# S5 states laid out by time, its input products side by side, its output weights in one half of the array

## The chip, the cores and the metric

The kernel runs on one core of a Trainium2 chip. The metric is the device time of one execution in microseconds (us). A core has a matrix engine (TensorE, PE in the profile), whose weight loads have a row of their own (PEld), a vector engine (DVE), a scalar engine (ACT), a general engine (POOL), and a queue engine (SP) that here only starts loads. Each engine takes its instructions strictly in the order of its own list, and waits when the next one's inputs or buffers are not ready.

## The reference, cut to what matters

Two identical layers run over 272 tokens (16 learned ones and 256 given) of width 2048. In each layer one input projection feeds three mixers: retention, gated linear attention (GLA) and S5. The change lies in the S5 branch alone, which is a complex recurrence over time:

```python
bu_re = jnp.einsum('blgc,gpc->blgp', ug, bb_re)
bu_im = jnp.einsum('blgc,gpc->blgp', ug, bb_im)
...
_, _, h_re, h_im = lax.associative_scan(complex_affine_combine, (a_re, a_im, bu_re, bu_im), axis=1)
y = jnp.einsum('blgp,gcp->blgc', h_re, c_re) - jnp.einsum('blgp,gcp->blgc', h_im, c_im)
return y.reshape(bsz, length, S5_WIDTH) + d * u
```

The index g runs over 64 groups of 16 channels, p over 64 complex states of a group, l over time.

## The kernel before

**Main products.** All large products are made from 656 chunks of weights (8 blocks of 128x128), which SP loads. ACT rounds a chunk to `hi` (L137), DVE makes the rest `lo` (L139), each with three buffers, and TensorE multiplies: L194, L195 and L196 in the first part of a layer, L191 and L196 where the activations' two halves are streamed together. A chunk is 24 products of the first kind. Every 16 or 8 weight blocks form one `acc` tile. These are called main products below.

**Order.** `schedule()` writes out the order of the output blocks by hand: GLA heads 0 and 1, the eight S5 input blocks (`su`), GLA heads 2 and 3, the retention heads (`rv`, `rk`, `rq`, `rg`), then gates and output. The smaller work is queued by `after(n, ...)`, which runs it n chunks later. A scheduler then places each engine's instructions, so what is traced together may stand apart on TensorE.

**S5.** Two time steps are folded into one, which leaves HALF = 136 steps, and two groups share the 128 partitions, which leaves 32 pairs. For each of the eight S5 blocks `s5_weights` turns the input weights (transposes into `tz`, copied out by ACT), and `s5_in` multiplies them with the inputs: 8 products for 4 pairs, each on 64 rows of the array (pr = 0 the lower half, pr = 1 the upper), into four PSUM tiles `s2p`. ACT copies each tile into the state tensor `H` (L537). When all of H is written, `s5_scan` runs the recurrence on POOL: 135 steps of three instructions, each on all 64 numbers (real and imaginary part of 32 pairs) of a partition: L543 multiplies the state of step n - 1 by the table `tab`, L545 and L546 add the two parts to step n. `s5_out` then multiplies H with the output weights `Ct`, 64 columns wide, into the PSUM tile `yp` (L558), behind one product with `K0` (L555); DVE adds the results to `su`. The scan has no other work in its way on POOL, and the products of `s5_out` stand in TensorE's list among the main products of the last retention heads.

`H` is [partition, time, re/im, pair] before. PSUM has five buffers for such small tiles (`patt`); `s2p`, `tz`, `yp`, and the small tiles of the other mixers share them.

Of the kernel before, what the change touches and what calls it, by code (L numbers as in the profile page):

```python
# [12 lines left out]
F32 = mybir.dt.float32  # L13
# [3 lines left out]
AF = mybir.ActivationFunctionType  # L17
ALU = mybir.AluOpType
# [4 lines left out]
P = 128  # L23
# [13 lines left out]
PAIRS = 32  # L37
HALF = T // 2
# [51 lines left out]
def hybrid(ctx: ExitStack, tc: tile.TileContext, xT, wst, wg, small, bcp, cst, rot, dec, out):  # L90
    nc = tc.nc
    V, S, G, PE = nc.vector, nc.scalar, nc.gpsimd, nc.tensor
# [3 lines left out]
    tp = ctx.enter_context(tc.tile_pool(name="tp", bufs=1))  # L96
# [6 lines left out]
    def nm(s):  # L103
        cnt[0] += 1
        return f"{s}_{cnt[0]}"

    def U(w=T):
        t = tp.tile([P, 288], F32, tag="u", name=nm("u"), bufs=NU)
        return t[:, :w]
# [4 lines left out]
    def PT(shape, s="att"):  # L114
        return patt.tile(shape, F32, tag="att", name=nm(s))
# [4 lines left out]
    def sm(l, n, i=None):  # L120
        a, b = SMALL[n]
        return smalls[l][:, a:b] if i is None else smalls[l][:, a + i:a + i + 1]
# [25 lines left out]
    def after(n, fn):  # L148

        cnt[0] += 1  # L150
        lag.append((state["t"] + n, cnt[0], fn))
# [22 lines left out]
    def bg_finish(g):  # L174
        if g in bg:
            for _ in g:
                pass
            bg.remove(g)

    def block(mv, nk, c0, wide=False):  # L180
        ps = pacc.tile([P, 512], F32, tag="acc", name=nm("acc"))
        w = T - c0
        both = wide and 2 * w <= 512
        for hc in range(nk // 8):
            prefetch(AHEAD + 1)
            hi, lo = chunks.popleft()
            for k in range(8):
                kk = hc * 8 + k
                o = ps[:, 0:w]
                if both:  # L190
                    PE.matmul(ps[:, 0:2 * w].rearrange("p (j t) -> p j t", j=2), hi[:, k, :], mv[:, :, kk, c0:T],  # L191
                              start=(kk == 0), stop=False, skip_group_check=True)
                else:
                    PE.matmul(o, hi[:, k, :], mv[:, 0, kk, c0:T], start=(kk == 0), stop=False)  # L194
                    PE.matmul(o, hi[:, k, :], mv[:, 1, kk, c0:T], start=False, stop=False)  # L195
                PE.matmul(o, lo[:, k, :], mv[:, 0, kk, c0:T], start=False, stop=(kk == nk - 1),  # L196
                          skip_group_check=both)
            bg_step()
        if both:
            z = U(w)  # L200
            S.activation(z, ps[:, w:2 * w], AF.Copy)
            V.tensor_tensor(out=ps[:, 0:w], in0=ps[:, 0:w], in1=z, op=ALU.add)
        return ps[:, 0:w]
# [90 lines left out]
    for d in range(0, KT, 4):  # L294
        if d < 12:
            tc.keep_in_program_order(S.activation(sq[:, d:d + 4, :], h0[:, d:d + 4, :], AF.Square))
        else:
            tc.keep_in_program_order(V.tensor_tensor(out=sq[:, d:d + 4, :], in0=h0[:, d:d + 4, :],
                                                     in1=h0[:, d:d + 4, :], op=ALU.mult))
# [24 lines left out]
    e = 1  # L324
# [3 lines left out]
    for l in range(DEPTH):  # L328
# [33 lines left out]
        s5 = {}  # L362
# [149 lines left out]
        su = tp.tile([P, NB, 2, HALF], F32, tag="su", name=nm("su"))  # L512
# [14 lines left out]
        def s5_in(b, u2):  # L527
            H = s5["H"]
            s2s = [PT([P, 2, HALF], "s2p") for _ in range(4)]
            for v_ in range(2):  # L530
                for ri in range(2):
                    for pr in range(2):
                        h_ = slice(64 * pr, 64 * pr + 64)
                        PE.matmul(s2s[2 * v_ + pr][:, ri, :], s5["ts", b][v_][h_, ri, :], u2[h_, v_, :], start=True,
                                  stop=True)
            for j, s2 in enumerate(s2s):
                S.activation(H[:, :, :, 4 * b + j].rearrange("p n r -> p r n"), s2, AF.Copy)  # L537

        def s5_scan():
            H, tab = s5["H"], s5["tab"]  # L540
            for n in range(1, HALF):
                pr = tp.tile([P, 2, 2, PAIRS], F32, tag="pr", name=nm("pr"), bufs=2)
                G.tensor_tensor(out=pr, in0=H[:, n - 1].unsqueeze(1).broadcast_to([P, 2, 2, PAIRS]),  # L543
                                in1=tab.rearrange("p (k r) q -> p k r q", k=2), op=ALU.mult)
                G.tensor_tensor(out=H[:, n], in0=H[:, n], in1=pr[:, 0], op=ALU.add)  # L545
                G.tensor_tensor(out=H[:, n], in0=H[:, n], in1=pr[:, 1, ::-1, :], op=ALU.add)  # L546
                if n % 2 == 0:
                    yield

        n0 = c0 // 2  # L550

        def s5_out(b):
            H, Ct, K0 = s5["H"], s5["C"], s5["K0"]
            yp = PT([P, 3, HALF], "yp")
            PE.matmul(yp[:, 2, n0:], K0[:, b, :], su[:, b, 0, n0:], start=True, stop=True, skip_group_check=True)  # L555
            m0 = max(n0 - 1, 0)
            for ri, q in ((0, 0), (0, 1), (1, 0), (1, 1), (0, 2), (0, 3), (1, 2), (1, 3)):
                PE.matmul(yp[64 * (q % 2):64 * (q % 2) + 64, q // 2, m0:],  # L558
                          Ct[:, ri, 4 * b + q].rearrange("p e a b -> p (e a b)"), H[:, m0:, ri, 4 * b + q],
                          start=(ri == 0), stop=(ri == 1), tile_position=(0, 64 * (q % 2)), skip_group_check=True)  # L560
            so = su[:, b, 0, n0:]
            V.scalar_tensor_tensor(out=so, in0=so, scalar=sm(l, "d", b), in1=yp[:, 2, n0:], op0=ALU.mult, op1=ALU.add)
            a = max(n0, 1)
            for q in range(4):
                r_, c_ = slice(32 * q, 32 * q + 32), 64 * (q % 2)
                so = su[r_, b, 1, n0:]
                V.scalar_tensor_tensor(out=so, in0=so, scalar=sm(l, "d", b)[r_], in1=yp[c_:c_ + 32, q // 2, n0:],
                                       op0=ALU.mult, op1=ALU.add)
                so = su[r_, b, 0, a:]
                V.tensor_tensor(out=so, in0=so, in1=yp[c_ + 32:c_ + 64, q // 2, a - 1:HALF - 1], op=ALU.add)  # L570
            so = su[:, b, :, n0:]
            S.activation(so, so, AF.Gelu_apprx_tanh)

# [191 lines left out]
        for kind, i, nk in schedule():  # L765
# [19 lines left out]
            elif kind == "su":  # L785
                if i == 0:
                    bg_finish(prep)
                    s5["H"] = tp.tile([P, HALF, 2, PAIRS], F32, tag="big", name=nm("H"))
                ps = block(x, nk, 0)
                V.tensor_tensor(out=su[:, i], in0=ps.rearrange("p (n e) -> p e n", e=2),  # L790
                                in1=R.rearrange("p (n e) -> p e n", e=2), op=ALU.mult)
                u2 = U().rearrange("p (a b) -> p a b", a=2)
                for v_ in range(2):
                    for pr in range(2):
                        for e in range(2):
                            G.dma_start(out=u2[64 * pr + 32 * e:64 * pr + 32 * e + 32, v_, :],  # L796
                                        in_=su[64 * v_ + 32 * pr:64 * v_ + 32 * pr + 32, i, e, :])
                after(3, partial(s5_weights, i))
                after(5, partial(s5_in, i, u2))
                if i == NB - 1:  # L800
                    scan = s5_scan()
                    after(6, partial(bg.append, scan))
            elif kind == "rv":
                if i == 0:
                    s2 = tp.tile([P, 2, NB, T], F32R, tag="s2", name=nm("ro"))
# [11 lines left out]
            elif kind == "rg":  # L817
                z = gate(block(x, nk, c0))
                after(5, partial(lambda z, rl, i: gated(z, rl["n"], s2, i), z, rl, i))
                if i == RH - 2:  # L820
                    after(6, partial(bg_finish, scan))
                    for b in range(NB):
                        after(6 + 3 * b // 2, partial(s5_out, b))
            elif kind == "sg":
# [9 lines left out]
                if i >= 4:  # L834
                    for b in (2 * i - 8, 2 * i - 7):
                        so_split(b)
                        so = su[:, b, :, n0:]
                        G.tensor_tensor(out=so, in0=so, in1=sgs[b][:, c0:].rearrange("p (n e) -> p e n", e=2),
                                        op=ALU.mult)
            elif kind == "glu":  # L840
                if i == 0:
# [4 lines left out]
                                in1=z[:, c0:].rearrange("p (n e) -> p e n", e=2), op=ALU.mult)  # L846
# [47 lines left out]
        else:  # L894
# [3 lines left out]
            r = U()  # L898
# [88 lines left out]
```

## Time and profile before

| what | value |
|---|---|
| time of three runs | 2164.37, 2166.74, 2167.22 us (median 2166.74) |
| profiled execution: time, and span of its instructions | 2164.37 us, 2162.6 us |
| TensorE's mean granted clock | 0.996 of full speed |
| busy: PE, DVE, ACT, POOL | 99%, 66%, 48%, 32% of the span |
| POOL, the three instructions of the scan | 457.7 us in all (169.6 + 152.1 + 136.0) |

The profiled execution is one of the three. TensorE's products are pipelined: in the rows, a product's duration includes its passage through the array, so that the next one begins long before it ends. What a product costs is read from the distance of the starts. A product of plain fp32 data (all of S5) shows as two passes, that is two records.

### The profile page before, as it was taken

How to read it: one execution, taken by the hardware profiler on the slowest of the kernel's cores; microseconds unless marked ns; L12 is line 12 of the kernel's file. 1: busy time of each engine (PE TensorE's matmuls, PEld its weight loads, DVE VectorE, ACT ScalarE, POOL GpSimd, SP SyncE). 2: the span in 40 equal slices, each digit the busy share in tenths (PEclk: the TensorE clock that was granted, in tenths of full speed). 3: DMA queues.
4: the chain of work that ended last, by engine and by line, in shares of the span. 5: the costliest groups of instructions: out<-in, count | busy, mean ns of one | idle time of the engine just before them, and what ended most of it. 6: DMA issues, size and time to landing. Idle time of an engine off the chain costs nothing. (4 is left out here: it accounts for less than half of the span.)

```text
span 2162.6 us, 39822 instructions
## 1 busy us (share of the span) xinstructions
PE 2140.4 (99%) x15650; PEld 2010.5 (93%) x15650; DVE 1434.2 (66%) x2370; ACT 1039.5 (48%) x1516; POOL 696.9 (32%) x1111
## 2 busy tenths in 40 slices
PE   9999999999999999999999999999999999999997
PEld 8999999998999999999999999999978888888886
DVE  7943788887555555555668636888886666666655
ACT  6655444446434444434445555444365444445454
POOL 3153888841200000002321428888603000000022
PEclk9999999999999999999999999999999999999999
DMA  6343444443555555545654434444435555555564
GB/s 225 141 156 120 153 165 161 161 147 106 178 176 176 176 174 174 173 173 192 213 204 149 150 125 160 163 170 163 152 109 184 190 189 187 191 187 188 191 212 152
DMA packets 108412, 365.47 MB, mean 169 GB/s; under 512 B 14016, under 2 KB 21696, under 8 KB 107968
## 3 DMA queue, kind: packets, MB, share of 16 engines
q1 hardware_dynamic: 101536, 353.73, 47.6%
q0 software_dynamic: 6400, 8.92, 1.3%
q8 instruction: 123, 2.02, 0.4%
q14 instruction: 65, 0.53, 0.1%
q10 hardware_dynamic: 288, 0.27, 0.1%
HBM read 356.32 MB, written 4.33 MB: 167 GB/s over the span
## 5 line engine op out<-in xcount | busy, mean ns | idle before, releaser
L137 ACT ACTIVATE hi<-raw 128x1024 fp32r<-128x1024 f32 x656 | 695.3, 1060 | 947.3 <-PE acc L195 533.0
L139 DVE TENSOR_TENSOR lo<-raw,hi 128x1024 fp32r<-128x1024 f32 x656 | 823.6, 1256 | 464.2 <-ACT hi L137 455.5
L196 PE MATMUL acc<-x,lo 128*128 128x272 f32 (+1 forms) x3840 | 1103.1, 287 | 1.1 <-DVE lo L139 1.1
L194 PE MATMUL acc<-x,hi 128*128 128x272 f32 (+1 forms) x2944 | 856.1, 291 | 1.1 <-ACT hi L137 1.1
L195 PE MATMUL acc<-x,hi 128*128 128x272 f32 (+1 forms) x2944 | 849.6, 289 | 0.0
L196 PEld LDWEIGHTS acc<-x,lo 128*128 128x128 f32 x3840 | 722.9, 188 | 4.3 <-DVE lo L139 1.5
L194 PEld LDWEIGHTS acc<-x,hi 128*128 128x128 f32 x2944 | 555.0, 189 | 11.8 <-issue 7.4
L195 PEld LDWEIGHTS acc<-x,hi 128*128 128x128 f32 x2944 | 555.2, 189 | 2.8
L191 PE MATMUL acc<-x,hi 128*128 128x512 f32 x896 | 316.0, 393 | 0.2 <-ACT u L756 0.2
L860 POOL TENSOR_TENSOR u<-u,u 128x272 f32<-128x272 f32 (+1 forms) x32 | 24.2, 755 | 768.2 <-DVE u L856 743.8
L191 PEld LDWEIGHTS acc<-x,hi 128*128 128x128 f32 x896 | 168.1, 188 | 41.2 <-issue 2.6
L543 POOL TENSOR_TENSOR pr<-H,tab 128x128 f32<-128x128 f32 x270 | 169.6, 628 | 78.6 <-ACT H L537 57.6
L545 POOL TENSOR_TENSOR H<-H,pr 128x64 f32<-128x64 f32 x270 | 152.1, 563 | 21.2
L196 PE MATMUL acc<-y,lo 128*128 128x272 f32 (+1 forms) x512 | 145.7, 285 | 0.0
L546 POOL TENSOR_TENSOR H<-H,pr 128x64 f32<-128x64 f32 x270 | 136.0, 504 | 21.2
L196 PEld LDWEIGHTS acc<-y,lo 128*128 128x128 f32 x512 | 96.3, 188 | 0.4
L191 PE MATMUL acc<-y,hi 128*128 128x512 f32 x240 | 83.8, 393 | 0.0
L796 POOL DMA_DIRECT2D u<-su x128 | 63.0, 500 | 52.6 <-ACT hi L137 31.5
L194 PE MATMUL acc<-y,hi 128*128 128x272 f32 (+1 forms) x272 | 78.4, 288 | 0.0
L195 PE MATMUL acc<-y,hi 128*128 128x272 f32 (+1 forms) x272 | 78.2, 288 | 0.0
L196 PE MATMUL acc<-ro,lo 128*128 128x272 f32 (+1 forms) x256 | 72.9, 285 | 0.0
L196 PE MATMUL acc<-go,lo 128*128 128x272 f32 (+1 forms) x256 | 72.9, 285 | 0.0
(285 smaller groups left out, 2726.2 us busy)
## 6 DMA issues: line engine op xcount, KB each, us to landing
raw<-wst SPq DMA_DIRECT2D x656, 512.0 KB, 3.3
h<-xT SPq DMA_DIRECT2D x8, 272.0 KB, 5.6
u<-su POOLq DMA_DIRECT2D x128, 17.0 KB, 2.5
u<-dec SPq DMA_DIRECT2D x16, 136.0 KB, 3.3
u<-xT POOLq DMA_DIRECT2D x16, 136.0 KB, 2.5
h<-u POOLq DMA_DIRECT2D x16, 136.0 KB, 2.2
u<-h POOLq DMA_DIRECT2D x16, 136.0 KB, 4.3
pre<-bcp SPq DMA_DIRECT2D x2, 1024.0 KB, 8.1
```

The source lines that it names most:

```text
L137: S.activation(hi, raw, AF.Copy)
L139: V.tensor_tensor(out=lo, in0=raw, in1=hi.bitcast(F32), op=ALU.subtract)
L191: PE.matmul(ps[:, 0:2 * w].rearrange("p (j t) -> p j t", j=2), hi[:, k, :], mv[:, :, kk, c0:T], start=(kk == 0), stop=False, skip_group_ch ...
L194: PE.matmul(o, hi[:, k, :], mv[:, 0, kk, c0:T], start=(kk == 0), stop=False)
L195: PE.matmul(o, hi[:, k, :], mv[:, 1, kk, c0:T], start=False, stop=False)
L196: PE.matmul(o, lo[:, k, :], mv[:, 0, kk, c0:T], start=False, stop=(kk == nk - 1), skip_group_check=both)
L543: G.tensor_tensor(out=pr, in0=H[:, n - 1].unsqueeze(1).broadcast_to([P, 2, 2, PAIRS]), in1=tab.rearrange("p (k r) q -> p k r q", k=2), op= ...
L545: G.tensor_tensor(out=H[:, n], in0=H[:, n], in1=pr[:, 0], op=ALU.add)
L546: G.tensor_tensor(out=H[:, n], in0=H[:, n], in1=pr[:, 1, ::-1, :], op=ALU.add)
L796: G.dma_start(out=u2[64 * pr + 32 * e:64 * pr + 32 * e + 32, v_, :], in_=su[64 * v_ + 32 * pr:64 * v_ + 32 * pr + 32, i, e, :])
L860: G.tensor_tensor(out=t[:, c0:], in0=t[:, c0:], in1=mg["y"][:, c0:], op=ALU.add)
```

## The change

In the S5 branch:

- `H` becomes [partition, re/im, pair, time], so that the 136 steps of one pair lie side by side, and the 64 numbers of one step lie 544 bytes apart (136 x 4). ACT's copies, the scan and the output products read and write it in that form.
- `s5_in` goes through v, ri, pr in another order (the upper row half first), and each product is pinned behind the one before it, so that the eight stand together on TensorE. `s5_weights` is queued one chunk earlier.
- `s5_out` takes two PSUM tiles instead of one. All its output weights go to columns 0 to 63 of the array; before, two of four pairs used columns 64 to 127.

```diff
-            for v_ in range(2):
-                for ri in range(2):
-                    for pr in range(2):
-                        h_ = slice(64 * pr, 64 * pr + 64)
-                        PE.matmul(s2s[2 * v_ + pr][:, ri, :], s5["ts", b][v_][h_, ri, :], u2[h_, v_, :], start=True,
-                                  stop=True)
+            for j, (v_, ri, pr) in enumerate((v_, ri, pr) for v_ in (1, 0) for ri in (0, 1) for pr in (1, 0)):
+                h_ = slice(64 * pr, 64 * pr + 64)
+                mm = PE.matmul(s2s[2 * v_ + pr][:, ri, :], s5["ts", b][v_][h_, ri, :], u2[h_, v_, :], start=True, stop=True)
+                if j:
+                    tc.keep_in_program_order(mm)
             for j, s2 in enumerate(s2s):
-                S.activation(H[:, :, :, 4 * b + j].rearrange("p n r -> p r n"), s2, AF.Copy)
+                S.activation(H[:, :, 4 * b + j, :], s2, AF.Copy)
...
-                G.tensor_tensor(out=pr, in0=H[:, n - 1].unsqueeze(1).broadcast_to([P, 2, 2, PAIRS]),
+                G.tensor_tensor(out=pr, in0=H[:, :, :, n - 1].unsqueeze(1).broadcast_to([P, 2, 2, PAIRS]),
                                 in1=tab.rearrange("p (k r) q -> p k r q", k=2), op=ALU.mult)
-                G.tensor_tensor(out=H[:, n], in0=H[:, n], in1=pr[:, 0], op=ALU.add)
-                G.tensor_tensor(out=H[:, n], in0=H[:, n], in1=pr[:, 1, ::-1, :], op=ALU.add)
+                G.tensor_tensor(out=H[:, :, :, n], in0=H[:, :, :, n], in1=pr[:, 0], op=ALU.add)
+                G.tensor_tensor(out=H[:, :, :, n], in0=H[:, :, :, n], in1=pr[:, 1, ::-1, :], op=ALU.add)
...
-            for ri, q in ((0, 0), (0, 1), (1, 0), (1, 1), (0, 2), (0, 3), (1, 2), (1, 3)):
-                PE.matmul(yp[64 * (q % 2):64 * (q % 2) + 64, q // 2, m0:],
-                          Ct[:, ri, 4 * b + q].rearrange("p e a b -> p (e a b)"), H[:, m0:, ri, 4 * b + q],
-                          start=(ri == 0), stop=(ri == 1), tile_position=(0, 64 * (q % 2)), skip_group_check=True)
+            for q in range(4):
+                for ri in range(2):
+                    PE.matmul(yps[q // 2][0:64, q % 2, m0:], Ct[:, ri, 4 * b + q].rearrange("p e a b -> p (e a b)"),
+                              H[:, ri, 4 * b + q, m0:], start=(ri == 0), stop=(ri == 1), skip_group_check=True)
...
-                    s5["H"] = tp.tile([P, HALF, 2, PAIRS], F32, tag="big", name=nm("H"))
+                    s5["H"] = tp.tile([P, 2, PAIRS, HALF], F32, tag="big", name=nm("H"))
...
-                after(3, partial(s5_weights, i))
+                after(2, partial(s5_weights, i))
```

On TensorE, the second S5 block of the first layer stood like this before; `s2p` is the result of `s5_in`, the second operand `u` its weights, `acc` rows are main products:

```order
L194 MATMUL acc_1816<-x_83,hi_1722 128x272
L534 MATMUL s2p_1750<-u_1529,u_1672 128x136
L534 MATMUL s2p_1751<-u_1529,u_1672 128x136
L534 MATMUL s2p_1750<-u_1529,u_1672 128x136
L534 MATMUL s2p_1751<-u_1529,u_1672 128x136
L195 MATMUL acc_1816<-x_83,hi_1722 128x272
L196 MATMUL acc_1816<-x_83,lo_1724 128x272
L194 MATMUL acc_1816<-x_83,hi_1722 128x272
L195 MATMUL acc_1816<-x_83,hi_1722 128x272
L534 MATMUL s2p_1752<-u_1529,u_1677 128x136 x2
```

Six of the block's eight products are seen: four with the row halves in turn, and two of one row half after four main products; the last two follow 15 main products later. The same block now (the products' line has moved up by two):

```order
L195 MATMUL acc_1826<-x_83,hi_1778 128x272
L532 MATMUL s2p_1763<-u_1539,u_1620 128x136
L532 MATMUL s2p_1762<-u_1539,u_1620 128x136
L532 MATMUL s2p_1763<-u_1539,u_1620 128x136
L532 MATMUL s2p_1762<-u_1539,u_1620 128x136
L532 MATMUL s2p_1761<-u_1539,u_1615 128x136
L532 MATMUL s2p_1760<-u_1539,u_1615 128x136
L532 MATMUL s2p_1761<-u_1539,u_1615 128x136
L532 MATMUL s2p_1760<-u_1539,u_1615 128x136
L521 MATMUL tz_1806<-cs,Z_871 128x128 x2
L196 MATMUL acc_1826<-x_83,lo_1780 128x272
```

All eight stand together, the row halves in turn. The last block of such products stands 12 main products later than its last piece did in the first layer (behind 1140 of them instead of 1128), and 13 later in the second (9016 instead of 9003); the second pair of transposes for the next block follows 12 main products behind each group.

The first output products of the first layer on TensorE, before:

```order
L196 MATMUL acc_5996<-x_83,lo_5964 128x272
L555 MATMUL yp_6060<-su_235,K_107_1363 128x136
L558 MATMUL yp_6060<-H_1372,C_1106 64x136 x8
L194 MATMUL acc_6086<-x_83,hi_5999 128x272
L195 MATMUL acc_6086<-x_83,hi_5999 128x272
```

And now:

```order
L196 MATMUL acc_5996<-x_83,lo_5964 128x272
L554 MATMUL yp_6060<-su_235,K_107_1363 128x136
L558 MATMUL yp_6060<-H_1372,C_1106 64x136 x4
L558 MATMUL yp_6061<-H_1372,C_1106 64x136 x4
L194 MATMUL acc_6087<-x_83,hi_5999 128x272
```

They have not moved: 3024 main products of the kernel stand ahead of them in both orders, and 10896 ahead of the second layer's. POOL's list is the same in both: the scan's rows follow the same transfers.

## Rows read from the trace of the kernel before

**Rows 1.** The page's first part: busy time of TensorE, share of the span.

```profile
PE 2140.4 (99%) x15650; PEld 2010.5 (93%) x15650; DVE 1434.2 (66%) x2370; ACT 1039.5 (48%) x1516; POOL 696.9 (32%) x1111
```

**Rows 2.** Timeline of PE: start, length, line, operation, count; an input burst of four passes.

```profile
124.70 0.29 PE L194 MATMUL acc<-x,hi 128*128 128x272 f32 x1
...
124.95 0.29 PE L196 MATMUL acc<-x,lo 128*128 128x272 f32 x1
125.17 0.73 PE L534 MATMUL s2p<-u,u 64*128 64x136 f32 x4
125.82 0.39 PE L194 MATMUL acc<-x,hi 128*128 128x272 f32 x1
126.06 0.29 PE L195 MATMUL acc<-x,hi 128*128 128x272 f32 x1
```

**Rows 3.** Timeline of PE: an input burst of eight passes.

```profile
138.14 0.73 PE L534 MATMUL s2p<-u,u 64*128 64x136 f32 x8
139.03 0.29 PE L196 MATMUL acc<-x,lo 128*128 128x272 f32 x1
```

**Rows 4.** Line L534: passes, shortest/median/longest ns, first and last start.

```profile
L534 PE MATMUL s2p<-u,u x256: 276/276/380, 125.2 to 1292.5; 64*128 64x136 f32 x128
```

**Rows 5.** Timeline of PE: the first output block of the first layer.

```profile
467.92 0.39 PE L555 MATMUL yp<-su,K 128*128 128x136 f32 x2
468.24 2.63 PE L558 MATMUL yp<-H,C 128*64 128x136 f32 x16
470.81 0.39 PE L194 MATMUL acc<-x,hi 128*128 128x272 f32 x1
```

**Rows 6.** Timeline of PE: the first two output blocks of the second layer.

```profile
1553.02 0.38 PE L555 MATMUL yp<-su,K 128*128 128x128 f32 x2
1555.62 2.51 PE L558 MATMUL yp<-H,C 128*64 128x129 f32 x16 [2.21 <-POOL H L546]
1558.06 0.58 PE L194 MATMUL acc<-x,hi 128*128 128x256 f32 x1
...
1561.79 2.51 PE L558 MATMUL yp<-H,C 128*64 128x129 f32 x16
1564.23 0.39 PE L194 MATMUL acc<-x,hi 128*128 128x256 f32 x1
```

**Rows 7.** Windows behind that wait: length, busy times, granted clock (PEclk), DMA.

```profile
1555.70:1559.10 3.40, 3.40 (x21) 2.52 (x22) 2.63 (x7) 0.00 (x0) 0.00 (x0) 0.51 0.52 181
1559.20:1565.00 5.80, 5.80 (x45) 4.51 (x44) 4.72 (x12) 3.11 (x4) 0.00 (x0) 1.00 0.10 39
```

**Rows 8.** The scan's three lines: count, shortest/median/longest ns, first and last start.

```profile
L543 POOL TENSOR_TENSOR pr<-H,tab x270: 453/464/1586, 199.7 to 1554.3; 128x128 f32<-128x128 f32 x135
L545 POOL TENSOR_TENSOR H<-H,pr x270: 317/325/1805, 200.7 to 1554.8; 128x64 f32<-128x64 f32 x135
L546 POOL TENSOR_TENSOR H<-H,pr x270: 317/324/1772, 201.1 to 1555.2; 128x64 f32<-128x64 f32 x135
```

**Rows 9.** Timeline of POOL: two neighbours, the first layer's last, the second's first.

```profile
300.24 0.33 POOL L546 TENSOR_TENSOR H<-H,pr 128x64 f32<-128x64 f32 x1
300.65 0.46 POOL L543 TENSOR_TENSOR pr<-H,tab 128x128 f32<-128x128 f32 x1
...
458.42 0.32 POOL L546 TENSOR_TENSOR H<-H,pr 128x64 f32<-128x64 f32 x1
...
1293.66 0.73 POOL L543 TENSOR_TENSOR pr<-H,tab 128x128 f32<-128x128 f32 x1 [29.62 <-ACT H L537]
```

**Rows 10.** Window over the first scan, of line L139 (`lo`) alone: DVE busy, count.

```profile
199.60:458.80 259.20, 99.95 (x76) 1.00 0.46 158
```

**Rows 11.** Groups of ACT by line: count, busy us, mean ns of one, idle before.

```profile
L137 ACT ACTIVATE hi<-raw 128x1024 fp32r<-128x1024 f32 x656 | 695.3, 1060 | 947.3 <-PE acc L195 533.0 <-issue 204.4 <-PE acc L191 189.3
L537 ACT ACTIVATE H<-s2p 128x272 f32<-128x272 f32 x64 | 40.4, 667 | 29.3 <-PE s2p L534 28.8
L523 ACT ACTIVATE u<-tz 128x256 f32<-128x256 f32 x32 | 11.1, 399 | 0.0
```

More of the change, by code (lines that the diff above doesn't have):

```diff
@@ L553, in s5_out @@
             H, Ct, K0 = s5["H"], s5["C"], s5["K0"]
-            yp = PT([P, 3, HALF], "yp")
-            PE.matmul(yp[:, 2, n0:], K0[:, b, :], su[:, b, 0, n0:], start=True, stop=True, skip_group_check=True)
+            yps = [PT([P, 3, HALF], "yp") for _ in range(2)]
+            PE.matmul(yps[0][:, 2, n0:], K0[:, b, :], su[:, b, 0, n0:], start=True, stop=True, skip_group_check=True)
             m0 = max(n0 - 1, 0)
-            for ri, q in ((0, 0), (0, 1), (1, 0), (1, 1), (0, 2), (0, 3), (1, 2), (1, 3)):
-                PE.matmul(yp[64 * (q % 2):64 * (q % 2) + 64, q // 2, m0:],
-                          Ct[:, ri, 4 * b + q].rearrange("p e a b -> p (e a b)"), H[:, m0:, ri, 4 * b + q],
-                          start=(ri == 0), stop=(ri == 1), tile_position=(0, 64 * (q % 2)), skip_group_check=True)
+            for q in range(4):
+                for ri in range(2):
+                    PE.matmul(yps[q // 2][0:64, q % 2, m0:], Ct[:, ri, 4 * b + q].rearrange("p e a b -> p (e a b)"),
+                              H[:, ri, 4 * b + q, m0:], start=(ri == 0), stop=(ri == 1), skip_group_check=True)
             so = su[:, b, 0, n0:]
-            V.scalar_tensor_tensor(out=so, in0=so, scalar=sm(l, "d", b), in1=yp[:, 2, n0:], op0=ALU.mult, op1=ALU.add)
+            V.scalar_tensor_tensor(out=so, in0=so, scalar=sm(l, "d", b), in1=yps[0][:, 2, n0:], op0=ALU.mult, op1=ALU.add)
             a = max(n0, 1)
             for q in range(4):
-                r_, c_ = slice(32 * q, 32 * q + 32), 64 * (q % 2)
+                r_, yp = slice(32 * q, 32 * q + 32), yps[q // 2][:, q % 2]
                 so = su[r_, b, 1, n0:]
-                V.scalar_tensor_tensor(out=so, in0=so, scalar=sm(l, "d", b)[r_], in1=yp[c_:c_ + 32, q // 2, n0:],
+                V.scalar_tensor_tensor(out=so, in0=so, scalar=sm(l, "d", b)[r_], in1=yp[0:32, n0:],
                                        op0=ALU.mult, op1=ALU.add)
                 so = su[r_, b, 0, a:]
-                V.tensor_tensor(out=so, in0=so, in1=yp[c_ + 32:c_ + 64, q // 2, a - 1:HALF - 1], op=ALU.add)
+                V.tensor_tensor(out=so, in0=so, in1=yp[32:64, a - 1:HALF - 1], op=ALU.add)
             so = su[:, b, :, n0:]
```

## The prediction

> **What bounds the kernel now.** I read the page's busy times first: TensorE is busy for 99% of the span [rows 1], so whatever its list loses or gains is the time, unless it is made to wait. Next came its timeline around the S5 products, to see what they cost between main products, which follow each other every 0.125 us (124.70 to 124.95 with one between) [rows 2]. Third, the list of who waited for whom and the rows behind it: TensorE waits once for the scan on POOL, 2.21 us in the second layer [rows 6]. The scan itself waits for nothing between its first and last instruction: neighbours are 0.08 us apart (300.24 + 0.33 to 300.65) [rows 9]. It runs from 199.7 to 458.74 in the first layer (259 us) and from 1293.66 to 1555.6 in the second (262 us) [rows 8, 9]; the output products want it at 468.24 and at 1553.4 [rows 5, 6]. So POOL is idle for two thirds of the span and yet has 9.5 us to spare in one layer and none in the other. That is what decides here.
>
> **Gain 1: the input products.** A burst of four passes on one row half takes 0.89 us from its first start to the second main product behind it (125.17 to 126.06) [rows 2]; a burst of eight with the halves in turn takes the same 0.89 (138.14 to 139.03) [rows 3], so the two halves work at once. Against the two main products' steps it would hold anyway, a burst costs 126.06 - 124.95 - 0.25 = 0.86 us [rows 2]. Four steps of 0.116 are in it (0.73 less the 0.276 of the last pass [rows 4], less the slower first step, over the rest); the other 0.39 is the way in and out, paid per burst. The 256 passes [rows 4] stand in 53 bursts, 42 of four and 11 of eight, counted over the timeline: 53 x 0.855 = 45.3 us. Now there are 16 bursts of 16 passes, eight pairs each: 0.86 + 4 x 0.116 = 1.33 us, 21.2 us in all. **Gain 24.1 us.** The transposes moved one chunk earlier stay the same transposes; the second pair of each block needs a PSUM tile that ACT's first copy of H frees, and 12 main products (1.5 us) stand ahead of it as cover, against one copy of about 0.4 us and at worst one `hi` of 1.06 us ahead of that [rows 11]. Without cover it would be 14 waits of up to 1 us; I take 0.
>
> **Gain 2: the output products.** Two passes of 64 columns run at once, eight pairs from 468.24 to 470.81: 2.57 us, 0.30 per pair and a way out [rows 5]. The K0 product, whose right side lies unbroken in SBUF, does a pass of the same length in 0.39 - 0.276 = 0.115 us [rows 4, 5]. [...] With H unbroken, 16 passes one after the other: 15 x 0.115 + 0.20 for the way out (as behind the input bursts: 125.17 + 0.73 - 0.276 to 125.82 [rows 2, 4]) = 1.93 us, or 1.80 with the second layer's shorter passes (0.38 for two K0 passes [rows 6]) against 2.44. **Gain 16 x 0.64 = 10.2 us.** If 64 columns no longer cost a way in and out, 0.29 us more per block, 4.6 in all.
>
> [...]
>
> **Off the path.** ACT's copies of H take 0.667 us each with their steps of 256 bytes; copies of the same kind out of `tz` take 0.399 for 256 elements, so 0.41 for 272 by the slope of `hi` ((1060 - 399) / 768 = 0.86 ns) [rows 11]. 64 x 0.25 us of ACT are saved, on an engine that waits for TensorE. DVE reads the same sizes from two tiles. Neither sets the end.
>
> **Loss: the scan.** POOL's scan starts when the last copy of H is done [rows 9], and I let TensorE's clock of main products tell what it has. The last input group stands 12 (13) main products later, 1.5 us, and is longer, with four copies behind it: I estimate that the scan starts 3 us after that burst's start, where it was 1.8 us. From scan start to `s5_out` this leaves 266 us in the first layer (268.5 before) and 257 in the second (259.7 before).
>
> A step of the scan is 0.464 + 0.325 + 0.324 by the medians [rows 8] and three gaps of 0.08: 1.35 us, 182 us for 135. The other 77 and 80 us are the long ones (up to 1.8 us), which I put down to DVE's `lo` operations, 76 in the first scan [rows 10], about 1 us each. So POOL has 182/259 = 0.703 and 182/262 = 0.696 of the time for itself, and within 266 and 257 us it can do 187 and 179 us of work. When TensorE waits, `lo` stops for want of buffers, and the rest runs free.
>
> Now each step reads H one number at a time, 544 bytes apart: 128 reads in L543 (each state twice) and 64 each in the two adds, 256 in all; 128 writes too. The trace has no such POOL instruction. Bounds per strided element: nothing at all; ACT's strided copy, (667 - 414) / 272 = 0.93 ns [rows 11]; TensorE's strided pass, (0.30 - 0.115) / 136 = 1.35 ns [rows 5]. I take ACT's for the reads, since ACT, like POOL in its adds, goes through a partition's numbers one after the other (0.86 ns each, and POOL 2.2, below), and hide the writes behind them: 256 x 0.93 = 0.238 us a step, 135 x 1.585 = 214 us of work. TensorE then waits 214 - 187 = 27 us in the first layer and 214 - 179 = 35 in the second, 62, of which 2.2 are there already. Behind L558 stands every main product, in order, and `hi` and `lo` can run three chunks ahead at most, so nothing is made up. Behind the 2.21 us wait the clock was 0.51 for 3.4 us [rows 7], which costs 1.7 us of main work; before, most of that fell on passes that did not care, about 0.6 lost. Twice 1.7 less 0.6: 2.8 more. **Loss 62.1 - 2.2 + 2.8 = 62.7 us.**
>
> [...]
>
> **Sum.** On the profiled execution: 2164.4 - 24.1 - 10.2 + 62.7 = 2192.8 us (its span and the 1.8 us around it move together). That execution is the fastest of the three, 2.4 us under the median; on the median the same +28.4 gives **2195 us**. The loss is 0.27 us per ns of a step's lengthening, less 0.9: it equals the 34.3 of gain at 130 ns a step, 0.51 ns per strided read. A change of 0.2% (4.3 us) is about what can be told from none here.
>
> **Rivals.**
> R1, faster: POOL pays nothing for the steps. For it: two contiguous inputs already take it (464 - 325) / 64 = 2.2 ns an element [rows 8], and a strided stream of ACT's pace, about 2 ns an element ((667 - 125) / 272, with 125 as the fixed part by the slope above), would fit beside that if POOL fetches its two inputs at once. Against it: both other engines that touch H in steps slow down, and an engine that reads its two inputs in turn adds the price. Then TensorE waits 182 - 179 = 3 us in the second layer and none in the first: 2166.7 - 34.3 + 2.2 = 2135 us. It decides below 0.51 ns a read.
> R2, near no change: POOL pays about half, 0.4 to 0.6 ns: 2159 to 2174 us.
> R3, slower by TensorE: the passes keep 0.30 us although alone on one column half. Then s5_out costs 15 x 0.30 + 0.20 - 2.57 = 2.1 us more a block, 34 instead of -10, and with the scan's price 2239 us; without it 2179. [...]
> R4, slower still: strided writes cost as much as reads and do not hide, at 0.93 ns 384 x 0.93 = 0.357 us a step: 2227 us (at 1.35 ns, 2271).
>
> **How the numbers follow.** Forecast case, POOL pays 0.7 ns a read or more (2180 to 2225, the upper end at 1.35 ns): 0.55. R4 and R3 together 0.09. R1 with prices up to 0.4 ns, 0.29. R2 0.07, of which 0.04 lies within 0.2%, the rest split to either side, 0.02 faster and 0.01 slower. So faster 0.31, same 0.04, slower 0.65. The range must take in R1, since cases of both signs are likely; its lower end is R1's 2135 less the 4.6 of the way in and out, 2130. It ends at 2225 and leaves R4 and R3 mostly out. The likeliest case's own range is 2180 to 2225.
>
> **What would show each step.** Input products: 16 bursts of 16 passes, 1.3 us each, and no 0.89 us bursts. Output products: passes 0.115 us apart, 1.9 us a block. The scan's medians: 0.464 to about 0.58, 0.325 to about 0.38, and waits of TensorE for the scan's last add of some 27 and 35 us, with a granted clock near 0.5 for some us behind it. Wrong would be: scan medians unchanged (then R1), passes at 0.30 (R3), or waits for PSUM at the transposes.

## The result, and the profile after

The changed kernel takes 2186.8 us (median of 4 runs, 2186.51 to 2187.12), the kernel before 2166.8 us on the same chip (2164.37 to 2167.22). The ratio is 1.0095, with a 95% interval of 1.0079 to 1.0111: **slower by 0.95%**. The forecast was slower, 2195 us. The profiled execution took 2187.05 us, 22.7 us more than the profiled one of before.

Where these 22.7 us arise is read from main products, which both kernels run in the same order: the start of the same main product is looked up in both timelines, and the differences are taken.

| main product of that number | what lies behind it | after less before, us |
|---|---|---|
| 700 | nothing of the change yet | +0.25 |
| 1150 | first layer's input products | -11.3 |
| 3020 | last one ahead of the first output block | -11.1 |
| 3030 | the first output block | +13.6 |
| 3300 | all eight output blocks | +9.6 |
| 8600 | rest of the layer, start of the second | +10.0 |
| 9030 | second layer's input products | -2.8 |
| 10890 | ahead of its first output block | -2.1 |
| 10900 | that block | +25.2 |
| 11100 | all eight | +21.5 |
| end | | +22.7 |

So the input products gave back 11.6 and 12.8 us, the first output block of each layer lost 24.7 and 27.3, and the other seven blocks gave back 4.0 and 3.7. The remaining 2.8 are a slow drift elsewhere, whose cause was not looked for.

The page's first part for the changed kernel, as in [rows 1]:

```profile
PE 2114.1 (97%) x15650; PEld 2010.3 (92%) x15650; DVE 1447.5 (66%) x2370; ACT 1023.1 (47%) x1516; POOL 753.4 (34%) x1111
```

TensorE is busy for 26 us less than in [rows 1], while the kernel is longer. POOL is busy for 56 us more, and still for only 34% of the span. TensorE's list of waits (engine, line, releaser: us in all, times, longest) names the place:

```profile
PE yp L558 <- POOL H L545: 51.0, 2, 28.3
```

The timeline of TensorE, first an input group, then the first two output blocks of the first layer, then the first of the second layer, answers to [rows 2, 3, 5, 6]:

```profile
139.69 0.29 PE L195 MATMUL acc<-x,hi 128*128 128x272 f32 x1
139.91 1.20 PE L532 MATMUL s2p<-u,u 64*128 64x136 f32 x16
141.04 0.44 PE L521 MATMUL tz<-cs,Z 128*128 128x128 f32 x2
141.23 0.37 PE L196 MATMUL acc<-x,lo 128*128 128x272 f32 x1
141.44 0.29 PE L194 MATMUL acc<-x,hi 128*128 128x272 f32 x1
...
456.78 0.39 PE L554 MATMUL yp<-su,K 128*128 128x136 f32 x2
479.92 3.89 PE L558 MATMUL yp<-H,C 128*64 128x136 f32 x16 [22.75 <-POOL H L545]
483.74 0.60 PE L194 MATMUL acc<-x,hi 128*128 128x272 f32 x1
487.51 0.39 PE L554 MATMUL yp<-su,K 128*128 128x136 f32 x2
487.84 2.07 PE L558 MATMUL yp<-H,C 128*64 128x136 f32 x16
489.83 0.72 PE L724 MATMUL sc<-u,u 128*128 128x272 f32 x2
...
1579.59 3.70 PE L558 MATMUL yp<-H,C 128*64 128x129 f32 x16 [28.27 <-POOL H L545]
1583.22 0.58 PE L194 MATMUL acc<-x,hi 128*128 128x256 f32 x1
```

All eight input products of a block are one group of 16 passes. TensorE is ready for the output products at 457.2 and gets H at 479.9. The first block behind the wait takes 3.82 us (479.92 to 483.74), the next 1.99 (487.84 to 489.83), where [rows 5] had 2.57. The windows over the two waits and behind them (length, busy us of PE, PEld, DVE, ACT and POOL with counts, granted clock, DMA share, GB/s):

```profile
457.20:479.90 22.70, 0.00 (x0) 0.00 (x0) 3.94 (x7) 0.76 (x1) 19.22 (x45) 0.59 0.15 53
479.90:485.00 5.10, 5.08 (x21) 4.72 (x22) 2.48 (x8) 0.00 (x0) 0.00 (x0) 0.50 0.01 3
485.00:490.00 5.00, 5.00 (x40) 4.68 (x39) 2.83 (x7) 2.38 (x3) 0.00 (x0) 0.98 0.00 0
...
1551.30:1579.60 28.30, 0.03 (x2) 0.01 (x1) 3.70 (x7) 0.83 (x1) 23.94 (x56) 0.54 0.13 47
1579.60:1584.20 4.60, 4.60 (x20) 4.27 (x21) 2.10 (x7) 0.00 (x0) 0.00 (x0) 0.50 0.00 0
```

While TensorE stands, DVE stands too (3.94 of 22.7 us), and POOL alone works. Behind each wait the granted clock is 0.50 for some 5 us, and 0.98 in the window that follows the first. The scan's lines and ACT's copies of H (count, shortest/median/longest ns, first and last start; [rows 8, 11] before):

```profile
L536 ACT ACTIVATE H<-s2p x64: 391/401/419, 132.9 to 1291.9; 128x272 f32<-128x272 f32 x64
L542 POOL TENSOR_TENSOR pr<-H,tab x270: 511/560/2087, 189.9 to 1578.2; 128x128 f32<-128x128 f32 x135
L544 POOL TENSOR_TENSOR H<-H,pr x270: 349/431/1752, 190.5 to 1578.8; 128x64 f32<-128x64 f32 x135
L545 POOL TENSOR_TENSOR H<-H,pr x270: 351/387/1812, 190.9 to 1579.2; 128x64 f32<-128x64 f32 x135
```

The same lines within the first wait alone, where DVE is out of the way:

```profile
L542 POOL TENSOR_TENSOR pr<-H,tab x14: 512/512/1367, 458.5 to 478.5; 128x128 f32<-128x128 f32 x14
L544 POOL TENSOR_TENSOR H<-H,pr x15: 349/351/431, 457.5 to 479.1; 128x64 f32<-128x64 f32 x15
L545 POOL TENSOR_TENSOR H<-H,pr x15: 351/352/631, 458.0 to 479.5; 128x64 f32<-128x64 f32 x15
```

There the medians are nearly the shortest values: this is the scan's own pace, 0.512 + 0.351 + 0.352 and three gaps of 0.08, 1.45 us a step. Before, by the shortest values of [rows 8], it was 1.33 (0.453 + 0.317 + 0.317 and the gaps). From start to start, the shortest step takes 1.449 us, and 1.325 before: the strided reads cost 0.124 us a step in all.

### The profile page after: what moved, and what is told of

Read it like the earlier page. It is cut to its first block, busy times and chain, and to the rows that moved or that the text cites. A ratio compares the mean times of both kernels' runs of the same rounds, so it can differ in the third digit from the quotient of the medians.

```text
span 2185.3 us, 39796 instructions
## 1 busy us (share of the span) xinstructions
PE 2114.1 (97%) x15650; PEld 2010.3 (92%) x15650; DVE 1447.5 (66%) x2370; ACT 1023.1 (47%) x1516; POOL 753.4 (34%) x1111
## 5 line engine op out<-in xcount | busy, mean ns | idle before, releaser
L139 DVE TENSOR_TENSOR lo<-raw,hi 128x1024 fp32r<-128x1024 f32 x656 | 825.5, 1258 | 430.8 <-ACT hi L137 426.7
L542 POOL TENSOR_TENSOR pr<-H,tab 128x128 f32<-128x128 f32 x270 | 207.5, 769 | 71.0 <-ACT H L536 49.9
L544 POOL TENSOR_TENSOR H<-H,pr 128x64 f32<-128x64 f32 x270 | 161.8, 599 | 21.2
L545 POOL TENSOR_TENSOR H<-H,pr 128x64 f32<-128x64 f32 x270 | 144.4, 535 | 21.1
L558 PE MATMUL yp<-H,C 128*64 128x136 f32 (+1 forms) x256 | 35.9, 298 | 51.0 <-POOL H L545 51.0
L558 PEld LDWEIGHTS yp<-H,C 128*64 128x64 f32 x256 | 31.6, 148 | 53.2 <-POOL H L545 51.4
```

The source lines that it names most:

```text
L139: V.tensor_tensor(out=lo, in0=raw, in1=hi.bitcast(F32), op=ALU.subtract)
L542: G.tensor_tensor(out=pr, in0=H[:, :, :, n - 1].unsqueeze(1).broadcast_to([P, 2, 2, PAIRS]), in1=tab.rearrange("p (k r) q -> p k r q", k=2 ...
L544: G.tensor_tensor(out=H[:, :, :, n], in0=H[:, :, :, n], in1=pr[:, 0], op=ALU.add)
L545: G.tensor_tensor(out=H[:, :, :, n], in0=H[:, :, :, n], in1=pr[:, 1, ::-1, :], op=ALU.add)
L558: PE.matmul(yps[q // 2][0:64, q % 2, m0:], Ct[:, ri, 4 * b + q].rearrange("p e a b -> p (e a b)"), H[:, ri, 4 * b + q, m0:], start=(ri == ...
```

## The experiments

My theory (theory A in the expectations) was that H with its numbers 544 bytes apart slows POOL's reads, and that this alone makes the waits. Against it stood, in turn: that the pinned input products, or the scan's later start, bring part of them; that POOL pays for writes, or by distance. Of TensorE it was open what a pass costs by the layout of H and by the column halves.

**The input products alone.** The kernel before, with only this part of the change:

```diff
+            for j, (v_, ri, pr) in enumerate((v_, ri, pr) for v_ in (1, 0) for ri in (0, 1) for pr in (1, 0)):
...
+                if j:
+                    tc.keep_in_program_order(mm)
...
-                after(3, partial(s5_weights, i))
+                after(2, partial(s5_weights, i))
```

> Before, with the pinned input products alone (and the weights' transposes one chunk earlier); state layout and output products as before. Theory A (only the stepped reads of the scan on POOL cost time): the input products give 11.5 + 12.5 us as in the change, the scan keeps its 1.325 us a step and about 260 us, TensorE waits for it 0 us in the first layer and 4 to 6 in the second (2.2 before): 2145 to 2148 us, ratio 0.990 to 0.992. Rival B (the scan is late because the pinned groups stand later and fill ACT, whatever the layout): waits of 15 us or more here too, 2165 us or more.

Measured: 2144.81 us, 0.9905 [0.9891, 0.992]. The scan took 259.8 and 263.0 us, as before, and TensorE waited for it in the second layer only:

```profile
PE yp L557 <- POOL H L545: 5.8, 1, 5.8
```

This part is a gain by itself: 20.3 us, or 23.9 without the growth of the wait from 2.2 to 5.8. The waits of the changed kernel do not come from it. The other two parts of the change cost 42 us on top (2186.8 against 2144.81).

**The new layout alone.** The kernel before, with H in its new form and everything else old:

```diff
-                    s5["H"] = tp.tile([P, HALF, 2, PAIRS], F32, tag="big", name=nm("H"))
+                    s5["H"] = tp.tile([P, 2, PAIRS, HALF], F32, tag="big", name=nm("H"))
```

> Before with the new layout of H alone: input products not pinned, output products in both column halves. Theory A: output blocks 1.1 us instead of 2.57 (-23 us), the scan 285 to 290 us and waits of 18 to 24 and 24 to 28 us (2.2 before), half the clock behind both (+4): 2182 to 2196 us. Rival B (pinning is what delays the scan): waits below 10 us, 2150 us.

Measured: 2197.24 us in one run, 31.6 more than before on that chip and 1 us over the expectation. The scan took 290.2 and 287.6 us, and TensorE waited for it in both layers:

```profile
PE yp L558 <- POOL H L546: 48.1, 2, 26.8
```

With the old order and placing of all products the waits are there: the layout makes them.

**The scan on unbroken numbers, twice.** The changed kernel, in which the scan alone goes over other addresses, the 64 numbers of a step side by side, so that the recurrence is no longer computed. First forwards:

```diff
-                G.tensor_tensor(out=pr, in0=H[:, :, :, n - 1].unsqueeze(1).broadcast_to([P, 2, 2, PAIRS]),
+                G.tensor_tensor(out=pr, in0=F[:, n - 1].unsqueeze(1).broadcast_to([P, 2, 2, PAIRS]),
```

> The changed kernel, but the scan goes through H as if its 64 numbers of a step lay side by side; so it works on other numbers than the states (the recurrence is not computed), with the same instructions, order and sizes. Theory A: POOL's instructions go back to about 0.455, 0.318 and 0.318 us when nothing disturbs them, waits shrink from 22.7 and 28.3 us to 0 and 2 to 6, and the clock stays up: 2132 to 2140 us, ratio 0.984 to 0.988. Rival B (later start or more disturbance by DVE, not the steps): waits stay above 15 us, 2175 us or more.

Measured: 2129.98 us, 0.9838 [0.9822, 0.9855], under the expectation, and for a second reason that I had missed. The first numbers of this scan lie in what the first block's copies wrote, so it began at 134.4 instead of 189.9 and had 55 us more. That separates nothing. So once more, backwards, which needs the last copies first (`F[:, HALF - n]` and `F[:, HALF - 1 - n]`):

> As e2, the changed kernel with the scan going through H in unbroken pieces of 64 numbers (so not through the states; the recurrence is not computed), but backwards, so that its first step needs the last copies of H and starts where the changed kernel's does, which e2's did not. Theory A: 0.455, 0.318 and 0.318 us undisturbed, a scan of 257 to 264 us, waits of 0 and 3 to 7 us: 2131 to 2138 us, ratio 0.983 to 0.987. Rival B (start and disturbance, not the steps): the scan takes over 280 us again, 2170 us or more.

Measured: 2136.89 us, 0.9866 [0.9851, 0.988]. Two of the scan's lines, its first and last instruction in the first layer, and the wait:

```profile
L543 POOL TENSOR_TENSOR pr<-H,tab x270: 453/464/2078, 188.9 to 1527.3; 128x128 f32<-128x128 f32 x135
L545 POOL TENSOR_TENSOR H<-H,pr x270: 317/325/1782, 189.4 to 1527.8; 128x64 f32<-128x64 f32 x135
```

```profile
188.90 0.46 POOL L543 TENSOR_TENSOR pr<-H,tab 128x128 f32<-128x128 f32 x1 [24.03 <-ACT H L536]
...
447.05 0.32 POOL L546 TENSOR_TENSOR H<-H,pr 128x64 f32<-128x64 f32 x1
```

```profile
PE yp L559 <- POOL H L546: 4.4, 1, 4.4
```

It starts at 188.9, 1 us ahead of the changed kernel's, and takes 258.5 us instead of 290.0. The shortest values of [rows 8] are back, and 2186.8 - 2136.9 = 50 us are gone. The spacing of POOL's reads and writes is worth these 50 us, the lower clock behind the waits included.

**What in the spacing costs.** The changed kernel with the scan in four parts of 34 steps, on the last part of H: the numbers 4, 8 and 16 bytes apart, then read 544 bytes apart with the sums written unbroken to another tile:

```diff
+                s = (1, 2, 4, 136)[(n - 1) // 34]
```

> The changed kernel with the scan's 135 steps in four parts of 34: numbers 4, 8 and 16 bytes apart in the last part of H, then 544 bytes apart as in the change but with the sums written to a small unbroken tile (the recurrence is not computed in any part). Theory A with the price on reads beyond 8 bytes: undisturbed 0.455 and 0.318 at 4 and 8 bytes, 0.51 and 0.35 at 16 bytes, and the same 0.51 and 0.35 at 544 bytes with unbroken writes. Rival C (the price is on the stepped writes): the adds of the last part at 0.318. Rival D (a price that grows with the distance): 16 bytes between 0.455 and 0.49. The time, between the changed kernel and e5: 2145 to 2170 us.

Measured: 2132.51 us in one run, less than expected, since the output products no longer depend on most of what this scan writes; the durations are what counts. The multiplication by part (4, 8, 16, 544 bytes), then the first add in the last three:

```profile
L551 POOL TENSOR_TENSOR pr<-H,tab x34: 453/464/1418, 189.2 to 249.4; 128x128 f32<-128x128 f32 x34
L551 POOL TENSOR_TENSOR pr<-H,tab x34: 460/542/1412, 251.8 to 317.6; 128x128 f32<-128x128 f32 x34
L551 POOL TENSOR_TENSOR pr<-H,tab x35: 512/537/1898, 320.0 to 393.2; 128x128 f32<-128x128 f32 x35
L551 POOL TENSOR_TENSOR pr<-H,tab x32: 506/563/1532, 396.6 to 457.7; 128x128 f32<-128x128 f32 x32
...
L553 POOL TENSOR_TENSOR H<-H,pr x34: 321/328/1803, 252.4 to 319.0; 128x64 f32<-128x64 f32 x34
L553 POOL TENSOR_TENSOR H<-H,pr x34: 353/434/1582, 321.4 to 393.7; 128x64 f32<-128x64 f32 x34
L553 POOL TENSOR_TENSOR scr<-H,pr x32: 347/424/1718, 397.6 to 458.6; 128x64 f32<-128x64 f32 x32
```

The medians rise beside DVE's work: in the changed kernel the multiplication's is 556 ns ahead of the first wait and 512 within it, where DVE is out of the way. By the shortest values, 8 bytes cost 7 ns or less an instruction, 16 bytes 59 and 36, 544 bytes with unbroken writes about the same, 53 and 30. So reads pay, (512 - 453) / 128 = 0.46 ns and (353 - 317) / 64 = 0.56 ns each; writes and distance hardly do.

**The output products with the old layout.** The changed kernel with H as before:

> The changed kernel with H laid out as before (time outermost); output weights still in columns 0 to 63, two tiles. Theory A1 (a pass over H in steps of 256 bytes takes 0.30 us by itself): 16 passes one after the other take 4.7 us a block instead of 2.57, so 2.1 us more in each of 16 blocks against the old kernel, the scan as fast as before: 2166.8 - 24 + 3 + 34 = 2178 to 2182 us. Rival A2 (the pair of passes shared one fetch, each alone takes about 0.15): blocks as before, 2146 us.

Measured: 2164.22 us in one run. The block:

```profile
464.24 3.89 PE L558 MATMUL yp<-H,C 128*64 128x136 f32 x16
468.06 0.73 PE L724 MATMUL sc<-u,u 128*128 128x272 f32 x2
```

3.82 us for 16 passes are 0.24 each, the way in and out included. Neither of the two expected values was met. A pass that reads H in steps of 256 bytes takes 0.24 us alone, about twice an unbroken one (1.99 us for 16 in the changed kernel, 0.116 from start to start), and two in two column halves together take the 0.30 of [rows 5], so that the halves overlapped in part.

**The output products in both column halves.** The changed kernel, new layout, with the output products as before the change:

```diff
+                PE.matmul(yp[64 * (q % 2):64 * (q % 2) + 64, q // 2, m0:],
...
+                          start=(ri == 0), stop=(ri == 1), tile_position=(0, 64 * (q % 2)), skip_group_check=True)
```

> The changed kernel with the output products in both column halves, in pairs, and one PSUM tile, as before; H in the new layout. Theory A1: a pair takes 0.115 us as one pass does, 8 pairs and a way out 1.1 us a block instead of 1.93, so 0.8 to 0.9 us less in 16 blocks, the scan and its waits as in the change: 2172 to 2175 us. Rival A2 (two passes share one fetch): 0.23 a pair, no difference, 2187 us.

Measured: 2175.2 us in one run, 11.6 less than the changed kernel. The second block of the first layer:

```profile
485.89 1.15 PE L557 MATMUL yp<-H,C 128*64 128x136 f32 x16
486.97 0.40 PE L194 MATMUL acc<-x,hi 128*128 128x272 f32 x1
```

1.08 us a block where the changed kernel has 1.99. Less its first step (0.17) and its way out (0.21), as that block has them, six steps are left: an estimated 0.12 for a pair of passes, as for one (0.116). On unbroken H the two halves are worth nearly a factor of two, so that this part of the change throws away what its new layout had made possible. TensorE still waits 50.5 us for the scan.

**The scan's end met later.** The kernel of the last experiment, with four weight blocks of the second GLA head queued behind the S5 input blocks, so that the scan starts earlier, and its consumers four chunks later (`after(6, ...)` to `after(10, ...)`):

> e4 (new layout, pinned input products, both column halves) with more work between the scan's start and its use: the last four weight blocks of GLA head 1 come after the S5 input blocks instead of before (8 chunks), and the output products 4 chunks later. That gives the scan some 30 us more in the first layer and 28 in the second, where it lacked 23 and 28 and loses a third of what it gets to DVE. Theory A: no wait in the first layer, 0 to 10 us in the second: 2175 - 50 - 5 + 5 = 2118 to 2132 us, ratio 0.977 to 0.985. Rival E (TensorE only changes places with DVE or ACT as the one that is waited for, since the output blocks then fall into the gates' stage): 2145 us or more.

Measured: 2144.3 us, 0.9901 [0.9885, 0.9918]; expected was 2118 to 2132. TensorE no longer waits for the scan, which ends at 458.7, while the first output block stands at 482.1. But it waits at another place (timeline of TensorE, then the window around it, columns as above):

```profile
192.56 0.87 PE L637 MATMUL tr<-cs,u 128*128 128x128 f32 x3 [5.62 <-DVE u L667]
```

```profile
180.00:200.00 20.00, 14.38 (x97) 14.09 (x96) 15.58 (x29) 6.96 (x12) 17.57 (x32) 0.83 0.32 106
```

The moved blocks bring the end of their GLA head, a chain of ten DVE operations, in front of the next head's values (L667): in DVE's timeline they stand with four `lo` between 180.6 and 191.6, and L667 follows at 191.99. The scan runs beside them, since it begins at 167.0 now; what that adds was not separated. In the windows 100 to 200 and 1200 to 1300 us TensorE is busy for 92.9 and 91.6 of 100 us, against 100.0 and 99.1 in the experiment above. Of the 50.5 us of waits, 31 came back as time, some 15 turned up here, and the rest is open.

**Runs of two.** Both column halves, and H as [partition, re/im, pair/2, time, 2]: POOL finds two numbers side by side, and TensorE reads in steps of 8 bytes:

```diff
+ s5["H"] = tp.tile([P, 2, PAIRS // 2, HALF, 2], F32, tag="big", name=nm("H"))
```

> e4 (pinned input products, both column halves) with a third layout of H: partition, re/im, pair of pairs, time, two pairs. A step's 64 numbers lie in 32 runs of two (8 bytes), and the 136 steps of one pair lie 8 bytes apart, for POOL and for TensorE. Theory A, with e6's result that 8 bytes cost POOL nothing if a run of two is one fetch: 0.455, 0.318 and 0.318 us undisturbed, waits of 0 and 4 to 6 us, output blocks of 1.1 us if TensorE takes 8 bytes as well as it takes 4: 2119 to 2126 us, ratio 0.979 to 0.982. Rival F (each jump costs POOL, half of the numbers): about 0.48 and 0.335 us, waits of 8 and 14 us, 2142 us. Rival G (TensorE pays at 8 bytes too): 0.2 to 0.3 us a pair, 13 to 25 us more.

Measured: 2130.67 us, 0.9844 [0.9827, 0.986]. The multiplication, the first add and an output block:

```profile
L543 POOL TENSOR_TENSOR pr<-H,tab x270: 450/470/2067, 190.0 to 1526.6; 128x128 f32<-128x128 f32 x135
L546 POOL TENSOR_TENSOR H<-H,pr x270: 318/332/1807, 190.5 to 1527.1; 128x64 f32<-128x64 f32 x135
```

```profile
461.61 1.19 PE L561 MATMUL yp<-H,C 128*64 128x136 f32 x16
```

Undisturbed, either engine pays next to nothing now: POOL has the shortest values of [rows 8] again, and an output block takes 1.12 us where unbroken H took 1.08. The time missed the expected 2119 to 2126, since the scan still ended 8.0 us too late in the second layer. Against the 2.2 us of before, TensorE came to the output products 1.6 us earlier after the scan's start (258.1 against 259.7), and the scan itself took 4.1 us more (266.0 against 261.9), of which 1 us is found in the input products' experiment too (263.0). So runs of two are not quite free beside DVE's work; the first layer's scan took 260.6 us, where that experiment's took 259.8.

**Runs of two, met two chunks later.** The same with `after(8, ...)` and `after(8 + 3 * b // 2, ...)`:

> e9 with the output products two chunks (6 us) later in the order. Theory A: the rest of the wait in the second layer goes, with the half clock behind it: 5 to 9 us less than e9, 2112 to 2119 us. If e9 has rival F's waits: about 10 us less than e9.

Measured: 2124.59 us, 0.9815 [0.98, 0.983], 6 us less than the last and within the difference expected, though not the expected time. One wait of 2.8 us for the scan is left. It is the fastest version found, 40 us under the kernel before.

## Why the prediction was right, point by point

**What bounds the kernel.** Right: TensorE's list sets the time, and POOL, idle for two thirds of the span, has no slack where TensorE wants H.

**Gain 1.** Predicted 24.1 us, measured 11.6 + 12.8 = 24.4 in the table, and 23.9 in the first experiment. The groups, 16 of them, cost about 1.3 us each as worked out, and no wait for PSUM came at the transposes.

**Gain 2.** Predicted 10.2 us, measured about 8.8: 7.7 in fourteen blocks, 0.55 each, and as much taken for the two first ones apart from their clock. The passes are 0.116 apart as predicted, but a block takes 1.99 us instead of 1.93, or 1.90 instead of 1.80 in the second layer. That H's 256-byte steps, and not the array, made the old passes long, is what the runs show: 0.24 us alone with them, 0.116 without, and blocks of 2.44 us before the change at a granted clock of 0.51 as at 1.00 [rows 6, 7]. But what the two column halves are worth I judged by rows where H was the brake. Where it no longer is, a pair takes an estimated 0.12 us as one pass does, and 11.6 us were given away.

**Off the path.** ACT's copies take 0.401 us, predicted 0.41, and nothing of it reaches the end.

**Loss: the scan.** The mechanism and the place were right, the size was 62.7 us predicted and 53.1 measured: waits of 22.75 and 28.27 us (predicted 27 and 35), less the 2.2 of before, plus 4.3 for the clock. Two steps behind it were wrong, and against each other.

The first is the price, "I take ACT's for the reads", 0.93 ns. Measured are (512 - 454) / 128 = 0.45 and (351 - 317) / 64 = 0.53 ns, 0.124 us a step instead of 0.238. Writes cost next to nothing, as assumed: by the shortest values the first add takes 349 ns with its sums 544 bytes apart, and 347 with unbroken sums. The price comes between steps of 8 bytes and of 16: 460 and 512 ns.

The second is the constant share of time that POOL has for itself, "0.703 and 0.696". On the same footing (shortest values) it was 135 x 1.325 / 259 = 0.69 before. After, 121 steps began ahead of 458.5, where the 14 of the wait begin: 121 x 1.449 / (458.5 - 189.9) = 0.65. A step beside DVE's work went from 1.92 us (259 / 135) to 2.22 (268.6 / 121), by 0.30; a constant share would have made 0.18 of the 0.124 (0.124 / 0.69). With the measured price and the old share, the waits would be 195.6 - 0.69 x 267.3 = 11 us and 195.6 - 0.683 x 258.8 = 19 us, 30 in all; 51 were measured. The other 21 us are the fall of this share.

So by my own break-even of 130 ns a step the measured 124 would have come out at about no change: the sign was right because the disturbance grew with the strided reads. That it does is shown by the unbroken scan of nearly the same start, which takes 258.5 us. In the same stretch POOL is not hit more often, but harder. Into the stretch from 200.5 to 447 us fall 72 `lo` operations of DVE before the change and 73 after; 71 and 73 of POOL's scan instructions there take over 0.3 us more than the shortest of their line, all but one of them beside a `lo`. They lose 0.92 and 0.97 us each, and the others 10.8 and 15.0 us together. Why each disturbance costs POOL more when its reads are strided is open, and was not tried.

A price nearly twice too high stood in for a disturbance taken as constant: that the two errors nearly cancel, and so that the forecast came out 8 us from the measured time, is luck.

**The clock.** Predicted 2.8 us, measured about 4.3: the clock of 0.50 lasted from within each wait until 5.3 and 4.7 us behind it, where 3.4 had been read from a wait of 2.2 us [rows 7]. The first blocks, free of the 256-byte steps, now feel it as well: 3.82 us at 0.50 and 1.99 at 1.00 (487.8 to 489.8), where [rows 6, 7] had 2.44 at 0.51 and at 1.00.

**Sum.** -24.4 - 8.8 + 53.1, and 2.8 of drift that I had not foreseen, are the 22.7 of the profiled execution. Of the rivals, R1 falls by the reads' price, R3 by the passes, R4 by the unbroken writes. R2's price, half of ACT's, is the one that was met, without the time that I had given it, and the forecast case by its own words ("0.7 ns a read or more") did not come about.

## What to carry to other kernels

The layout that TensorE streams well (0.116 us a pass instead of 0.24) was paid for here by POOL, which walks the other axis (0.124 us a step); look for such an engine's slack at the point where its result is wanted, not in its share of busy time. Before choosing a side, try short runs that serve both: two numbers side by side cost either engine next to nothing here (450 ns a multiplication against 453, 1.12 us a block against 1.08), and took 44.5 us off (2175.2 to 2130.67, both with the two column halves). And when a price is added to an engine that a neighbour disturbs, measure a step beside that neighbour: here it grew by 0.30 us, for a price of 0.124 undisturbed.

## What the runs showed of the hardware

- Undisturbed, POOL's operations on two fp32 inputs pay about 0.5 ns for each number read in steps of 16 bytes, and no more at 544 (512 and 506 ns where unbroken reads take 453); at 8 bytes (460 ns), or in runs of two numbers with jumps between (450), next to nothing.
- Beside one of DVE's `lo` operations an instruction of POOL's scan lost about 0.92 us, and 0.97 with reads 544 bytes apart.
- An fp32 pass of TensorE over 136 columns takes 0.116 us with its moving side unbroken, and 0.24 in 256-byte steps (3.82 us for 16, against 1.99). Two such passes in two column halves together take an estimated 0.12 in the first case (1.08 us a block) and 0.30 in the second; in 8-byte steps, where only pairs were run, 0.12 by the same estimate (1.12 us a block).
- Passes that read in 256-byte steps, in two column halves, took the same time at a granted clock of 0.51 and of 1.00: 2.44 us a block [rows 6, 7]. An unbroken pass over 136 columns took twice as long at 0.50 (0.227 us, first block of the changed kernel) as at 1.00 (0.116, its second).
